# Attention scores of a two-layer decoder trunk: the matmuls of a row block regrouped by contraction depth

## The chip, the cores and the metric

The kernel runs on one core of a Trainium2 chip. The metric is the device time of one execution in microseconds (us), as the median of several runs.

## The reference, cut to what matters

Two layers work on x of 1024 tokens by 1024 features in float32. Layer 0 is a conformer convolution module with a gated feed-forward part; layer 1 is stick breaking attention with 16 heads of 64 features, then the same kind of feed-forward part. The change lies in the attention:

```
scale = 1 / sqrt(64); ts = arange(1024)
for each block of 128 queries, first query t0, for each head:
    z = einsum('qd,kd->qk', qblk, kh) * scale
    mask = ts[None, :] < (t0 + arange(128))[:, None]
    log_1m = where(mask, log_sigmoid(-z), 0)
    rev = cumsum of log_1m over later keys
    a = where(mask, exp(log_sigmoid(z) + rev - log_1m), 0)
    out = a @ v
```

## The kernel before, in words

To keep float32 accuracy, every operand of a matmul is split in a high and a low part. A product of a projection is three matmuls (`mm3`, L137 to L139): high by high, high by low, low by high. For the scores z, the queries of a head stand in one tile `q` of 128 partitions, the 64 high parts in one half, the 64 low parts in the other. The keys stand in `kh` (high parts in both halves) and in `kl` (low parts of both heads of a pair, each head in its own half). So one chunk of z, 128 queries by up to 512 keys, takes two matmuls on L739: one over 128 partitions (`q` by `kh`, both parts of q against the high part of k) and one over 64 partitions (the high half of `q` by `kl`). I call them the 128-row and the 64-row matmul. On the chunk with the diagonal a third one, L742, adds minus 1e30 where a key isn't earlier than its query; it multiplies two bfloat16 tiles of 128 by 128 (`identb`, `maskb`).

One call of `z_row` makes the scores of one block of 128 queries, in the tile `big` of two banks, 512 columns each. In the first half of the queries (blocks 0 to 3, up to 512 keys) it takes both heads of a pair, one bank for each: a two-head row. In the second half (blocks 4 to 7, 640 to 1024 keys) it takes one head with two chunks: a single-head row. There are 8 head pairs, so 32 two-head rows and 64 single-head rows. Behind the matmuls come two sigmoids on ScalarE (L755, L756), a scan over the keys on VectorE (L758) and a product on GpSimd (L760). `weigh` then transposes the weights on TensorE (L773), splits them into the tile `hl` (L776 and the helper L86; NH such tiles) and multiplies them with the values (L778, L779), which ends in `o` (L781, L782) and a store to DRAM (L800).

The work goes by units of a head pair and a half; the weighing runs two units behind the scores. The projections of the next head pair (L137 to L139) are put between as filling work, and in the last two steps the output projection `wo` of the first half. After the last unit, `wo` of the second half loads the stored results (L632), casts them (L633) and loads its weights (L130).

The order on each engine isn't written out by hand: a scheduler lays it out from the program with a timing model and packs the tiles into memory, so a change in one place can move instructions in the whole attention.

Of the kernel before, what the change touches and what calls it, by code (L numbers as in the profile page):

```python
# [15 lines left out]
DRAM = bass.MemoryType.DRAM  # L16

P = 128
# [3 lines left out]
HALF = 512  # L22
# [16 lines left out]
NM = 15  # L39
NH = 3  # L40
NX = 8
# [10 lines left out]
def trunk_kernel(ctx: ExitStack, tc, x, p, a_pw1_w, a_pw1_b, a_dw_w, a_dw_b, a_ln_g, a_ln_b, a_pw2_w, a_pw2_b,  # L52
# [37 lines left out]

    # ---------------------------------------------------------------- constants
    # one tile for all of them
    ctile = const.tile([P, 352], F32, name="ctile")
# [17 lines left out]
    class Rows:  # L111
        """Tiles of 4 KB, three to a slot."""

# [27 lines left out]
    def new_half():  # L141
        """High and low parts of a matrix (k, t) for the tokens of a half, in two tiles of four k blocks each."""
        return [[xtp.tile([P, 4, HALF], F32R, name="xT", align_bytes=A4) for _ in range(2)] for _ in range(2)]
# [20 lines left out]
    def ln_stats(src):  # L164
        nt = np_.tile([P, 24], F32, name="norm")
        st, mv, ve = nt[:, 0:12].rearrange("p (i s) -> p i s", i=2), nt[:, 12:14], nt[:, 14:16]
        rstd, tmp, nb = nt[:, 16:17], nt[:, 17:18], nt[:, 18:19]
        for i in range(2):
            nc.vector.bn_stats(out=st[:, i, :], in_=src[:, i * HALF:(i + 1) * HALF])
        nc.vector.bn_aggr(out=mv, in_=st)  # L170
        # reciprocal square root: a first guess from the exponent bits, then Newton steps to float32
        nc.vector.tensor_scalar(out=ve[:, 0:1], in0=mv[:, 1:2], scalar1=EPS, scalar2=None, op0=ALU.add)
        nc.vector.tensor_scalar(out=ve[:, 1:2], in0=mv[:, 1:2], scalar1=EPS, scalar2=-0.5, op0=ALU.add, op1=ALU.mult)
        nc.vector.tensor_scalar(out=tmp.bitcast(I32), in0=ve[:, 0:1].bitcast(I32), scalar1=1, scalar2=None,
                                op0=ALU.logical_shift_right)
        nc.vector.tensor_scalar(out=rstd.bitcast(I32), in0=tmp.bitcast(I32), scalar1=-1.0, scalar2=float(0x5f3759df),
                                op0=ALU.mult, op1=ALU.add)
        for _ in range(3):
            nc.vector.scalar_tensor_tensor(out=tmp, in0=rstd, scalar=ve[:, 1:2], in1=rstd, op0=ALU.mult, op1=ALU.mult)
            nc.vector.scalar_tensor_tensor(out=rstd, in0=tmp, scalar=1.5, in1=rstd, op0=ALU.add, op1=ALU.mult)  # L180
        return mv, rstd, nb
# [11 lines left out]

    # ---------------------------------------------------------------- p @ ple_w_proj, kept in DRAM until it is needed
    def ple_proj(i, sb, dst):
        """Pieces of work that need no result of the trunk."""
        pT, ws = [], []
# [36 lines left out]

    # ---------------------------------------------------------------- conv gated FFN + per-layer embedding
    def ffn_phase(i, xT, res, pp, g, b, sb, finish):
# [35 lines left out]

        # Gate and up projection: (W11 W21; W12 W22) of the two k halves and two column tiles, times (x11 x12; x21 x22) of
        # the two k halves and token halves, in seven block products (Strassen's, in Winograd's form).
        (x11, x21), (x12, x22) = ([[part[b] for part in xT[half]] for b in range(2)] for half in range(2))
# [35 lines left out]
        def fast(w, f, quad):  # L311
            """The products of column tiles f and f + 1 with all tokens, each in two parts."""
            pa, pb, pc, pd = quad
# [70 lines left out]

        # two sets of four banks
        (b0, b2), (b1, b3) = ((t[:, 0:HALF], t[:, HALF:]) for t in (big(), big()))
# [18 lines left out]

    # ---------------------------------------------------------------- layer 0
    x2d_dram = dram.tile([S, D], F32, name="x2_dram")
# [4 lines left out]
    with ExitStack() as l0:  # L412
# [3 lines left out]
        with ExitStack() as ph:  # L416
# [43 lines left out]

            # pointwise 1, the gate, and the depthwise convolution as three half-rate ones of the even, the odd and
            # the summed tokens: y_even = E + O', y_odd = B - E - O with the taps of even, odd and both places
            HB = 15 + HALF
# [18 lines left out]
            def depthwise(c, hb):  # L482
                nc.vector.tensor_tensor(out=hb[:, 2, :], in0=hb[:, 0, :], in1=hb[:, 1, :], op=ALU.add)
                # both: ACT multiplies, Pool adds. Tap k of E, O and B reads 15 - k places back.
                pb = sb.tile([P, HALF], F32, name="pb", bufs=2)
# [26 lines left out]
                yv = y.rearrange("p (m a) -> p m a", a=2)  # L512
                # the bias: in B already; E + O' takes it here
                nc.vector.scalar_tensor_tensor(out=yv[:, :, 0], in0=e, scalar=vec_a[:, 16 + c:17 + c], in1=os_[:, 0:HALF],
# [104 lines left out]

    # ---------------------------------------------------------------- output projection  # L620
    res = [None] * 8
# [30 lines left out]

    # ---------------------------------------------------------------- stick breaking attention
    with ExitStack() as ph:
# [4 lines left out]
        nc.gpsimd.memset(maskb, 0.0)  # L659
        # row q, key j of the diagonal block: NEG where j >= q  # L660
        nc.gpsimd.affine_select(out=maskb, in_=maskb, pattern=[[-1, P]], compare_op=ALU.is_gt, fill=NEG,
# [13 lines left out]
        def proj_qk(w, hp, hd):  # L675
            """q: (high | low) parts over the partitions, the other way round for the odd head.
            k: high parts twice, low parts twice."""
            is_q = w is b_wq
# [25 lines left out]
        def proj_v(qt, vs):  # L704
            """Per head (high | low) parts side by side, the other way round for odd heads."""
            cs = slice(qt * 256, (qt + 1) * 256)
# [23 lines left out]

        def z_mm(ps, at, hd, s, qb):
            n = (qb + 1) * P
            q, qs = hd["q"][s], slice(qb * P, (qb + 1) * P)
            for c0 in range(0, n, HALF):
                w = max(256, min(HALF, n - c0))
                diag = n <= c0 + HALF
                m = sides(s)[0]
                for j, (ks, k) in enumerate(((slice(0, P), hd["kh"][s]), (m, hd["kl"][0]))):
                    nc.tensor.matmul(out=ps[:, at + c0:at + c0 + w], lhsT=q[ks, qs], rhs=k[ks, c0:c0 + w],  # L739
                                     start=(j == 0), stop=(j == 1 and not diag))  # L740
                if diag:
                    nc.tensor.matmul(out=ps[:, at + n - P:at + n], lhsT=identb, rhs=maskb, start=False, stop=True)  # L742

        def z_row(hd, ss, qb, a):
            """Weight of key j: sigmoid(z_j) times the product over later keys of 1 - sigmoid(z_i) = sigmoid(-z_i);
            in the last column both parts are the mask's: 0 and 1."""
            n = (qb + 1) * P
            m = len(ss)
            ps = z_bank()
            for i, s in enumerate(ss):  # L750
                z_mm(ps, i * HALF, hd, s, qb)
            r = sb.tile([P, S], F32, name="rr", bufs=2, align_bytes=A4)
            rv, zv = (t.rearrange("p (m n) -> p m n", m=m) for t in (r, ps))
            av = a.rearrange("p (m n) -> p m n", m=m)
            nc.scalar.activation(out=av[:, :, 0:n], in_=zv[:, :, 0:n], func=AF.Sigmoid)  # L755
            nc.scalar.activation(out=rv[:, :, 0:n], in_=zv[:, :, 0:n], func=AF.Sigmoid, scale=-1.0)  # L756
            for i in range(m):
                nc.vector.tensor_tensor_scan(out=rv[:, i, 1:n][:, ::-1], data0=rv[:, i, 1:n][:, ::-1],  # L758
                                             data1=zero.broadcast_to([P, n - 1]), initial=1.0, op0=ALU.mult, op1=ALU.add)
            nc.gpsimd.tensor_tensor(out=av[:, :, 0:n - 1], in0=av[:, :, 0:n - 1], in1=rv[:, :, 1:n], op=ALU.mult)  # L760
            return av

        def weigh(hp, half, s, i, rows, o):
            """Values weighted, for head s and the four query blocks of a half."""
            v = vs[hp][s]
# [46 lines left out]
        for piece in pieces(0):  # L812
            piece()
        # the first half's units end early: its output projection goes beside the last units of the second half
        units = [(hp, half, ss) for hp in range(HP - 2) for half, ss in ((0, (0, 1)), (1, (0,)), (1, (1,)))]
# [29 lines left out]

    # ---------------------------------------------------------------- norm, layer 1 FFN
    with ExitStack() as l1:
# [45 lines left out]
```

## Time and profile before

| | us |
|---|---|
| median of 3 runs | 2754.74 (2754.44 to 2757.61) |
| span of the profiled execution, first to last instruction | 2746.3 |
| TensorE matmuls busy (PE) | 2585.2, 94% of the span |
| VectorE (DVE) | 1774.6, 65% |
| GpSimd (POOL) | 1201.6, 44% |
| ScalarE (ACT) | 1046.4, 38% |

Of the profiled execution only the span is known; the median stands 8.4 us above it, which is taken as the time around the span. Matmuls are pipelined and their ends are modelled, so a busy PE is not one at its peak: how dense the work is must be read from the starts of matmuls and of weight loads (PEld). The attention takes the stretch from 1270 to 1845 us.

### The profile page before, as it was taken

What the parts mean: (1) busy time and instruction counts of PE and PEld (TensorE: products, weight loads), DVE (VectorE), ACT (ScalarE), POOL (GpSimd) and SP (SyncE); (2) the same over time, 40 slices, a digit from 0 to 9 for tenths busy, and PEclk for the clock granted to TensorE, in tenths of its full rate; (3) what the DMA queues carried; (4) which work ended last, traced back from release to release, by engine and by line L of the source; (5) the groups of instructions that cost most, each with busy time, mean ns of one, the idle gap of its engine ahead of it and who ended that gap; (6) DMA issues with size and microseconds to landing.
All of it is one profiled execution on the core that took longest, in us unless ns stands there. A gap on an engine that the chain in (4) does not pass through costs nothing.

```text
span 2746.3 us, 34172 instructions
## 1 busy us (share of the span) xinstructions
PE 2585.2 (94%) x13300; PEld 2153.5 (78%) x13300; DVE 1774.6 (65%) x2785; ACT 1046.4 (38%) x1621; POOL 1201.6 (44%) x793
## 2 busy tenths in 40 slices
PE   8996998999999999999999999898899999999995
PEld 6885888988878778878777777588798787877874
DVE  4999769366565565583556665766946655656558
ACT  4556533233233232324555555642323332323231
POOL 3998236534434333412333333354653343433344
PEclk9998999999999999999999999999999999999998
DMA  4114421211111111222110101232221111211121
GB/s 149 47 47 153 163 68 62 77 47 61 47 54 58 52 52 46 69 92 68 32 50 23 45 25 38 73 125 89 70 69 62 47 60 48 62 46 46 47 77 61
DMA packets 149085, 179.12 MB, mean 65 GB/s; under 512 B 6508, under 2 KB 125756, under 8 KB 148924
## 3 DMA queue, kind: packets, MB, share of 16 engines
q1 hardware_dynamic: 144316, 168.56, 19.2%
q10 hardware_dynamic: 4608, 8.39, 0.8%
q8 instruction: 104, 1.70, 0.3%
q14 instruction: 57, 0.47, 0.1%
HBM read 151.76 MB, written 20.97 MB: 63 GB/s over the span
## 4 chain that ended last, share of the span: by engine, by line
PE 68%; DVE 18%; POOL 4%; issue 3%; ACT 3%; DMA 3%; SPq 0%; POOLq 0%; DVEq 0%; ACTq 0%
PE bank L137 13%; PE bank L138 13%; PE bank L139 12%; PE big L137 7%; PE big L139 7%; PE big L138 7%; PE big L739 3%; POOL w L86 3%; DVE bank L502 2%; DVE bank L509 2%; DVE pt L282 1%; DMA w<-in_ffn_w_up 1%; PE more L778 1%; PE more L779 1%; PE bank L773 1%
## 5 line engine op out<-in xcount | busy, mean ns | idle before, releaser
L86 POOL TENSOR_TENSOR w<-w 128x512 fp32r<-128x512 f32 (+1 forms) x444 | 755.8, 1716 | 1086.9 <-ACT w L299 675.8
L137 PE MATMUL bank<-w,xT 128*128 128x256 f32 x1280 | 367.2, 289 | 29.8 <-ACT sg L258 22.7
L299 ACT CAST w<-w 128x512 fp32r<-128x512 f32 x308 | 180.1, 619 | 542.0 <-DVE w L294 147.6
L138 PE MATMUL bank<-w,xT 128*128 128x256 f32 x1280 | 366.1, 287 | 1.4 <-POOL w L86 1.4
L139 PE MATMUL bank<-w,xT 128*128 128x256 f32 x1280 | 365.9, 288 | 0.9 <-DVE xT L86 0.9
L760 POOL TENSOR_TENSOR res<-res,rr 128x639 f32<-128x639 f32 (+3 forms) x96 | 150.2, 1565 | 316.2 <-DVE rr L758 290.0
L758 DVE TENSOR_TENSOR_SCAN rr<-rr,ctile 128x127 f32<-128x127 f32 (+7 forms) x128 | 180.1, 1428 | 162.2 <-ACT rr L756 162.1
L137 PEld LDWEIGHTS bank<-w,xT 128*128 128x128 f32 x1280 | 248.9, 195 | 32.6 <-ACT sg L258 24.1
L138 PEld LDWEIGHTS bank<-w,xT 128*128 128x128 f32 x1280 | 249.8, 195 | 2.5 <-POOL w L86 2.1
L139 PEld LDWEIGHTS bank<-w,xT 128*128 128x128 f32 x1280 | 248.5, 195 | 1.9 <-DVE xT L86 1.5
L132 ACT CAST w<-w 128x1024 fp32r<-128x1024 f32 x136 | 142.6, 1049 | 240.5 <-PE bank L138 42.8
L137 PE MATMUL big<-xT,w 128*128 128x512 f32 x544 | 212.0, 390 | 0.0
L138 PE MATMUL big<-xT,w 128*128 128x512 f32 x544 | 211.9, 389 | 0.0
L139 PE MATMUL big<-xT,w 128*128 128x512 f32 x544 | 211.6, 389 | 0.0
L137 PE MATMUL bank<-xT,w 128*128 128x512 f32 x496 | 197.4, 398 | 0.7 <-DVE m L86 0.6
L139 PE MATMUL bank<-xT,w 128*128 128x512 f32 x496 | 196.0, 395 | 0.0
L138 PE MATMUL bank<-xT,w 128*128 128x512 f32 x496 | 195.7, 394 | 0.0
L294 DVE TENSOR_TENSOR w<-w 128x512 f32<-128x512 f32 x176 | 126.9, 741 | 100.2 <-POOL w L86 50.4
L383 DVE TENSOR_TENSOR m<-m,bank 128x512 f32<-128x512 f32 x192 | 128.8, 682 | 85.0 <-PE bank L139 84.9
L137 PE MATMUL bank<-w,f 128*128 128x512 f32 x448 | 170.5, 395 | 7.7 <-ACT f L366 4.3
L138 PE MATMUL bank<-w,f 128*128 128x512 f32 x448 | 176.1, 393 | 0.0
L139 PE MATMUL bank<-w,f 128*128 128x512 f32 x448 | 173.2, 390 | 0.0
(161 smaller groups left out, 5969.4 us busy)
## 6 DMA issues: line engine op xcount, KB each, us to landing
w<-in_ffn_w_gate SPq DMA_DIRECT2D x44, 512.0 KB
w<-in_ffn_w_up SPq DMA_DIRECT2D x44, 512.0 KB
w<-in_ffn_w_down SPq DMA_DIRECT2D x44, 512.0 KB
w<-in_a_pw_w SPq DMA_DIRECT2D x32, 512.0 KB
pp<-o ACTq DMA_DIRECT2D x32, 256.0 KB
w<-in_ple_w_gate SPq DMA_DIRECT2D x16, 512.0 KB
w<-pp SPq DMA_DIRECT2D x16, 512.0 KB
w<-in_b_wo SPq DMA_DIRECT2D x16, 512.0 KB
```

The lines of the kernel that those rows point to most:

```text
L86: eng.tensor_tensor(out=l, in0=full, in1=h.bitcast(F32), op=ALU.subtract)
L132: nc.scalar.copy(out=h[:, 0:n], in_=raw)
L137: nc.tensor.matmul(out=o, lhsT=sh, rhs=mh, start=first, stop=False)
L138: nc.tensor.matmul(out=o, lhsT=sh, rhs=ml, start=False, stop=False)
L139: nc.tensor.matmul(out=o, lhsT=sl, rhs=mh, start=False, stop=last)
L294: nc.vector.tensor_tensor(out=out, in0=a, in1=c, op=op)
L299: nc.scalar.copy(out=h, in_=full)
L383: nc.vector.tensor_tensor(out=rv, in0=rv, in1=ps, op=ALU.add)
L502: nc.vector.scalar_tensor_tensor(out=e, in0=v, scalar=w, in1=e, op0=ALU.mult, op1=ALU.add)
L739: nc.tensor.matmul(out=ps[:, at + c0:at + c0 + w], lhsT=q[ks, qs], rhs=k[ks, c0:c0 + w], start=(j == 0), stop=(j == 1 and not diag))
L758: nc.vector.tensor_tensor_scan(out=rv[:, i, 1:n][:, ::-1], data0=rv[:, i, 1:n][:, ::-1], data1=zero.broadcast_to([P, n - 1]), initial=1.0, ...
L760: nc.gpsimd.tensor_tensor(out=av[:, :, 0:n - 1], in0=av[:, :, 0:n - 1], in1=rv[:, :, 1:n], op=ALU.mult)
```

## The change: 128-row matmuls of a row block first, then the 64-row ones

`z_mm` is now called once for a row block and goes over its two chunks twice: first the 128-row matmul of each chunk, with the mask right behind it, then the 64-row matmul of each. The same matmuls are done, on the same data, into the same banks. NH, the number of `hl` tiles of 4 KB a partition, goes from 3 to 4. Comments also go; the lines after them move by one or two (L739 becomes L737 and L743, L742 becomes L740).

```diff
-NH = 3
+NH = 4
...
-        def z_mm(ps, at, hd, s, qb):
+        def z_mm(ps, hd, ss, qb):
+
             n = (qb + 1) * P
-            q, qs = hd["q"][s], slice(qb * P, (qb + 1) * P)
-            for c0 in range(0, n, HALF):
-                w = max(256, min(HALF, n - c0))
-                diag = n <= c0 + HALF
+            qs = slice(qb * P, (qb + 1) * P)
+            chunks = [(i * HALF, s, c0, max(256, min(HALF, n - c0))) for i, s in enumerate(ss) for c0 in range(0, n, HALF)]
+            for at, s, c0, w in chunks:
+                nc.tensor.matmul(out=ps[:, at + c0:at + c0 + w], lhsT=hd["q"][s][:, qs], rhs=hd["kh"][s][:, c0:c0 + w],
+                                 start=True, stop=False)
+                if n <= c0 + HALF:
+                    nc.tensor.matmul(out=ps[:, at + n - P:at + n], lhsT=identb, rhs=maskb, start=False, stop=False)
+            for at, s, c0, w in chunks:
                 m = sides(s)[0]
-                for j, (ks, k) in enumerate(((slice(0, P), hd["kh"][s]), (m, hd["kl"][0]))):
-                    nc.tensor.matmul(out=ps[:, at + c0:at + c0 + w], lhsT=q[ks, qs], rhs=k[ks, c0:c0 + w],
-                                     start=(j == 0), stop=(j == 1 and not diag))
-                if diag:
-                    nc.tensor.matmul(out=ps[:, at + n - P:at + n], lhsT=identb, rhs=maskb, start=False, stop=True)
+                nc.tensor.matmul(out=ps[:, at + c0:at + c0 + w], lhsT=hd["q"][s][m, qs], rhs=hd["kl"][0][m, c0:c0 + w],
+                                 start=False, stop=True)
...
-            for i, s in enumerate(ss):
-                z_mm(ps, i * HALF, hd, s, qb)
+            z_mm(ps, hd, ss, qb)
```

In the order of TensorE, a single-head row before (the first of 640 keys; `big_81` is the scores' tile, `m` the keys and queries, `masks` the two mask tiles) is this, where of each "x2" the first is the 128-row and the second the 64-row matmul:

```order
L773 MATMUL more_9492<-ctile,res 128x128
L739 MATMUL big_81<-m 128x512 x2
L739 MATMUL big_81<-m 128x256 x2
L742 LDWEIGHTS masks
L742 MATMUL big_81<-masks 128x128
L137 MATMUL bank_82<-w,xT 128x256
```

And the same row now:

```order
L774 MATMUL more_9492<-ctile,res 128x128
L737 MATMUL big_81<-m 128x512
L737 MATMUL big_81<-m 128x256
L740 LDWEIGHTS masks
L740 MATMUL big_81<-masks 128x128
L743 MATMUL big_81<-m 128x512
L743 MATMUL big_81<-m 128x256
L137 MATMUL bank_82<-w,xT 128x256
```

The two 64-row matmuls (L743) now stand behind each other, and the mask has moved ahead of them. A two-head row before (384 keys for each of two heads):

```order
L739 MATMUL big_81<-m 128x384 x2
L742 LDWEIGHTS masks
L742 MATMUL big_81<-masks 128x128
L739 MATMUL big_81<-m 128x384 x2
L742 LDWEIGHTS masks
L742 MATMUL big_81<-masks 128x128
L773 MATMUL bank_84<-ctile,res 128x128
```

And a two-head row now (256 keys):

```order
L737 MATMUL big_81<-m 128x256
L740 LDWEIGHTS masks
L740 MATMUL big_81<-masks 128x128
L737 MATMUL big_81<-m 128x256
L740 LDWEIGHTS masks
L740 MATMUL big_81<-masks 128x128
L743 MATMUL big_81<-m 128x256 x2
L137 MATMUL bank_83<-xT,w 128x512
```

Over the whole attention TensorE's order goes from a 128-row to a 64-row matmul or back 384 times before and 192 times now; all 192 64-row matmuls stand in 96 pairs, and nothing stands between the two of a pair. Between the last L779 and the first transposes of the next part (L152) stand 174 matmuls of `wo` before, and 112 now. At that place SP's queue held this before (L800 stores a unit's result, L632 loads the results of the second half back, L130 loads weights):

```order
L800 DMA o_dram_94<-o 64x512
L130 DMA w<-in_b_wo 128x4x256 x2
L800 DMA o_dram_94<-o 64x512
L632 DMA w<-o_dram_94 128x2x512 x4
L130 DMA w<-in_b_wo 128x4x256 x8
```

And now:

```order
L801 DMA o_dram_94<-o 64x512
L130 DMA w<-in_b_wo 128x4x256
L632 DMA w<-o_dram_94 128x2x512 x3
L801 DMA o_dram_94<-o 64x512
L632 DMA w<-o_dram_94 128x2x512
L130 DMA w<-in_b_wo 128x4x256 x8
```

Three of the four loads now stand ahead of the last store instead of behind it.

## Rows read from the trace of the kernel before

**Rows 1.** The page: the span, and busy time by engine.
```profile
span 2746.3 us, 34172 instructions
PE 2585.2 (94%) x13300; PEld 2153.5 (78%) x13300; DVE 1774.6 (65%) x2785; ACT 1046.4 (38%) x1621; POOL 1201.6 (44%) x793
```

**Rows 2.** Busy time in the attention: PE, PEld, DVE, ACT, POOL; granted clock, DMA.
```profile
1270.00:1845.00 575.00, 555.74 (x2952) 425.42 (x2951) 352.99 (x475) 315.76 (x552) 213.85 (x121) 0.97 0.17 50
```

**Rows 3.** Groups by form, attention, PE: count, busy us, mean ns, idle before.
```profile
L739 PE MATMUL big<-m 64*128 64x512 f32 x96 | 48.8, 508 | 0.0
L742 PE MATMUL big<-masks 128*128 128x128 bf16 x128 | 29.6, 231 | 0.0
L739 PE MATMUL big<-m 64*128 64x256 f32 x64 | 24.8, 387 | 0.0
L739 PE MATMUL big<-m 64*128 64x384 f32 x32 | 14.3, 447 | 0.0
```

**Rows 4.** Timeline of weight loads, a single-head row: start, us, idle before.
```profile
1512.13 0.19 PEld L739 LDWEIGHTS big<-m 128*128 128x128 f32 x1
1512.67 0.18 PEld L739 LDWEIGHTS big<-m 64*128 64x128 f32 x1 [0.35 <-issue]
1513.10 0.19 PEld L739 LDWEIGHTS big<-m 128*128 128x128 f32 x1 [0.24 <-issue]
1513.41 0.18 PEld L739 LDWEIGHTS big<-m 64*128 64x128 f32 x1
1513.72 0.10 PEld L742 LDWEIGHTS <-masks 128*128 128x128 bf16 x1
1513.85 0.19 PEld L137 LDWEIGHTS bank<-xT,w 128*128 128x128 f32 x1
```

**Rows 5.** Timeline of matmuls at three places: start and us.
```profile
1278.63 0.59 PE L739 MATMUL big<-m 128*128 128x256 f32 x2
...
1512.13 0.39 PE L138 MATMUL bank<-xT,w 128*128 128x512 f32 x1
1512.35 1.44 PE L739 MATMUL big<-m 128*128 128x512 f32 x4
...
1843.08 0.28 PE L779 MATMUL more<-hl,m 128*128 128x256 f32 x1
1843.20 0.22 PE L778 MATMUL more<-hl,m 128*128 128x128 f32 x1
1843.26 0.34 PE L139 MATMUL bank<-w,xT 128*128 128x256 f32 x1
```

**Rows 6.** Timeline of weight loads, end of the two-head row from 1278.63.
```profile
1279.15 0.51 PEld L739 LDWEIGHTS big<-m 128*128 128x128 f32 x2
1279.91 0.19 PEld L138 LDWEIGHTS bank<-xT,w 128*128 128x128 f32 x1
```

**Rows 7.** A late stretch: all engines as in rows 2; then L742 alone (PE, PEld).
```profile
1680.00:1820.00 140.00, 130.51 (x640) 93.35 (x638) 103.80 (x127) 87.60 (x150) 54.48 (x32) 0.95 0.27 85
1680.00:1820.00 140.00, 8.15 (x35) 3.36 (x35) 0.95 0.27 85
```

**Rows 8.** Waits in the attention: us in total, times, longest.
```profile
PE big L739 <- ACT rr L756: 5.2, 8, 1.3
PE more L773 <- DVE hl L86: 4.4, 4, 2.0
ACT hl L776 <- PE more L779: 0.3, 1, 0.3
```

**Rows 9.** Timeline at the hand-over to the next part: SP's queue and PE.
```profile
1845.63 0.45 SPq L800 DMA_DIRECT2D o_dram<-o  x1
...
1870.71 0.58 PE L137 MATMUL bank<-w,xT 128*128 128x256 f32 x1 [4.95 <-ACT xT L633]
```

**Rows 10.** A wait of PE, and the stretch behind it, as in rows 2.
```profile
1441.06 1.11 PE L773 MATMUL more<-ctile,res 128*128 128x128 f32 x4 [1.99 <-DVE hl L86]
...
1441.00:1444.40 3.40, 3.34 (x11) 2.85 (x12) 3.34 (x6) 2.29 (x4) 0.52 (x1) 0.51 0.57 155
```

## The prediction, made before the changed kernel ran

> **What bounds the kernel now.** I read the page first: PE is busy 94% of the span, the next engine 65% [rows 1]. An average over stages proves little, so I read the windows next: in the attention, where everything that changes lies, PE is busy 555.7 of 575 us, and no other engine reaches two thirds of the stretch [rows 2]. PE waits for others there only 19.3 us. So the stage is bound by how long PE takes for its list, and the question is how dense that list is. Busy time doesn't tell, since ends are modelled and records overlap; starts do.
>
> The third view is therefore the timeline, and its starts give a rhythm. A 512-column matmul starts 0.22 us after another one, a 256-column one passes the queue in 0.12, a 128-column one in 0.06 [rows 5]. In this rhythm the weight load of the next matmul starts together with the matmul before it: the load for the first score matmul starts at 1512.13, and so does the projection matmul ahead of it [rows 4, 5]. The load is thus hidden. At the 64-row matmuls it isn't. The row that starts at 1512.35 should load its first 64-row weights at 1512.35; the load starts at 1512.67, after 0.35 us in which the load queue did nothing and no engine was waited for [rows 4]. From there to the next load, of a 128-row matmul, it is 0.43 us instead of 0.22. I read this as a price for each change between 128 and 64 rows: the matmul under way first runs out (0.32 less 0.22, so 0.10), then the load stands bare. The second part follows from the step 1512.67 to 1513.10: 0.43 less 0.22 is 0.21, which is the bare load (0.11) and the running out at its end (0.10). A change costs 0.21 us.
>
> **The change part by part.** *A single-head row before.* From the first matmul at 1512.35 to 1513.85, where the load of the second following projection matmul starts and with it, by the rhythm, the first such matmul, 1.50 us pass [rows 4, 5]. Its work in the rhythm is two times 0.22, two times 0.12 and 0.06 for the mask, 0.74. So 0.76 us are lost: 0.10 ahead of the first 64-row load, 0.21, then 0.19 twice (steps of 0.31 for 0.12), and 0.07 at the mask, which takes 0.13 instead of 0.06.
>
> *The same row now.* The two 128-row matmuls and the mask follow each other in the rhythm. Then one change (0.10 run out, 0.11 bare load), the second 64-row matmul with its load hidden under the first, and one change back (0.10, 0.11): 0.42 lost. It saves 0.34 us, and 64 rows 21.8 us.
>
> *A two-head row.* Before it takes from 1278.63 to 1279.91, 1.28 us [rows 5, 6], for work of four times 0.12 and two times 0.06, 0.60; 0.68 are lost. Now 0.42 are lost for the two changes, and the second head's 128-row load (0.11) is hidden only by the first head's mask (0.06), 0.05 more. It saves 0.21, and 32 rows 6.7 us. I use this for all widths, as the prices don't depend on the columns. The counts are those of the groups: 96 + 64 + 32 = 192 matmuls of 64 rows, two to a row [rows 3].
>
> Together 28.5 us at full clock. The mean granted clock of the stretch is 0.97 [rows 2], where PE's own steps are longer by as much: 29.4 us.
>
> *What the trace of before doesn't show* is a 64-row matmul behind another. Below, the pair costs nothing beyond the rhythm, as I took it; above, it costs a full change (0.21) in each of 96 rows, 20.2 us, which would leave 9. I take the lower end, since the row nearest in kind, a 128-row matmul behind a 128-row one, hides its load fully [rows 4, 5]. The pair of a two-head row could also run side by side, since the two heads use different halves of the partitions and different banks: then the second matmul vanishes, 0.12 to 0.22 us in 32 rows, 4 to 7 us more. No row shows such an overlap; I leave it out of the sum and in the range.
>
> The Trainium skill speaks against the hidden load: TensorE: Matmul & The Clock Gate, Part 3, "What overlaps and what doesn't", says that a weight load overlaps a matmul in flight only when it goes to another group of rows. By that, the pairs of the single-head rows, which use the same rows, would each show one bare load. For 128-row matmuls the rows here show the contrary, since those loads overlap although they use the same rows; for 64-row pairs nothing shows it yet.
>
> *NH from 3 to 4.* ScalarE waited for a free `hl` tile (its cast behind the second value matmul) once, for 0.3 us [rows 8]. So the fourth tile gives between 0 and 0.3 us; I take 0. Its use, if any, is for the scheduler.
>
> *Waits that take back some of it.* PE gets ahead by 6% of the stage, the others don't. In the late stretch, where less projection work fills the gaps, PE is already idle 9.5 of 140 us, and 35 of the 128 masks, so some 27% of the rows (8 us of the gain), lie there [rows 7]. There the scores wait for the sigmoids to free the only tile `big` (5.2 us in the whole stage) and the transposes for VectorE (4.4) [rows 8]. Ends are 0 and 8 us lost; I take 3, because PE is still busy 93% there, nearer to bound than not.
>
> *The hand-over.* Behind the last unit, `wo` of the first half covers the store and the loading back. PE ran dry there for 4.95 us until a cast by L633 [rows 9]. Now 62 matmuls fewer stand in that cover (174 less 112), 62 times 0.12 or 7.4 us; on the other hand three of four loads no longer queue behind the store, which was issued at 1845.63 [rows 9]. The ends are 7.4 us lost and 5 won; I take 0, as the cast that ended the gap also had loads behind the store.
>
> The sum is 29.4 less 3, 26.4 us. Against the profiled execution: 2746.3 less 26.4 is 2719.9, plus 8.4 around the span is 2728. The median of the runs, 2754.7, less 26.4 gives the same.
>
> **The rivals.** *The pair's second load stays bare.* For it: it is unseen. Against it: 128-row pairs. If only the 64 single-head pairs pay a change, 64 times 0.21 is 13.4 us off: gain 13, 2742. This is what the page's sentence above comes to.
>
> *More than the sum.* The two-head pairs overlap (4 to 7 us), or the late waits don't grow and the denser list leaves fewer dips of the clock: gain 34 to 40, 2715 to 2721. For the first the rows say nothing. The same page, Part 3, "Measured speedup vs the span model", has small matmuls in different groups of rows run side by side; no row of this case shows it.
>
> *The scheduler's new order hands most of it back.* The order on all engines moves throughout the attention. If the late stretch keeps nothing (8 us) and the hand-over loses its 7.4, and some waits are new, the gain is 5 to 14: 2741 to 2750.
>
> *Slower: VectorE's order collides with the weighing.* VectorE works in order; when a long scan stands ahead of the subtraction that makes `hl`, PE's transposes wait for a bank. It happened at 1441.06: PE waited 1.99 us, and then ran 3.4 us at a granted clock of 0.51, the lower of its two levels (1.2 GHz against 2.4), which costs 1.7 us more [rows 10]. So one collision costs 3.7 us. It takes eight new ones, one for each head pair, to cancel 29 us; with twelve the kernel ends 15 us slower, 2770. Against it: in the whole stage such waits for VectorE came to 4.4 us in four places [rows 8], and VectorE is busy 61% of it [rows 2].
>
> **How the numbers follow.** The sum as it stands (gain 20 to 33, 2721 to 2734): 0.53. More than the sum: 0.16. The bare second load: 0.12. Handed back: 0.11. Slower: 0.05, and 0.03 for something that cancels to within 0.2%. That 0.2%, 5.5 us, is about what a measurement of this kernel can tell from no change. The range leaves out the top of the second case (0.04), most of the handed-back one beyond 2744 (0.08) and the last two (0.08), so it goes from 2715 to 2744. Of the handed-back case 0.03 lies inside 0.2%: faster 0.53 + 0.16 + 0.12 + 0.08 = 0.89, same 0.06, slower 0.05.
>
> **What would show it.** In the changed profile, a single-head row should go from its first matmul to the restart of the rhythm in 1.16 us instead of 1.50, with one stretch of idle loads ahead of the first L743 and none ahead of the second (about 0.22 or 0.12 after it, by its width). If the second L743 load comes 0.10 later than that, the first rival holds; if the two L743 of a two-head row start within a few hundredths of a us, they overlap. The idle time on the load queue put to "issue" should halve. PE's idle time in the attention (19.3 us) should grow by some 3 us; above 30 it has handed the gain back. A wait for `hl` in every head pair would mean the slower case, and it would make the prediction wrong, as would a gap over 12 us at the hand-over.

## The result, and the profile after

The changed kernel takes 2726.16 us (median of 4 runs, 2722.46 to 2726.38) against 2754.59 for the kernel before (4 runs, 2751.79 to 2757.61): a ratio of 0.9894, with a 95% interval of 0.988 to 0.9908, so 25 to 33 us faster. The profiled execution has a span of 2720.3 us (before 2746.3); it took 2722.46 us itself, so what lies around the span is some 2 us, not the 8.4 that I took the median's distance for. By the same 2 us the profiled execution of the kernel before took some 2748 us, less than each of its four runs; so the spans differ by 26.0 us and the medians by 28.4.

The page of the changed kernel: span, and busy time by engine (against [rows 1]).

```profile
span 2720.3 us, 34159 instructions
PE 2554.6 (94%) x13300; PEld 2149.7 (79%) x13300; DVE 1785.5 (66%) x2785; ACT 1045.9 (38%) x1621; POOL 1195.0 (44%) x793
```

PE is busy for 31 us less with as many matmuls as before, and its share of the span is the same 94%. The busy time in the attention of the changed kernel, columns as in [rows 2], then its late part, as in [rows 7]:

```profile
1270.00:1822.00 552.00, 527.79 (x3011) 425.90 (x3010) 361.59 (x477) 315.64 (x552) 211.19 (x121) 0.97 0.18 55
1680.00:1822.00 142.00, 128.76 (x779) 104.89 (x780) 107.02 (x136) 85.59 (x142) 61.31 (x34) 0.95 0.31 100
```

PE now idles 24.2 us in this stage (552 less 527.79) instead of 19.3. A single-head row of the changed kernel, first the timeline of weight loads, the counterpart of [rows 4]:

```profile
1362.10 0.41 PEld L737 LDWEIGHTS big<-m 128*128 128x128 f32 x2
1362.67 0.10 PEld L740 LDWEIGHTS <-masks 128*128 128x128 bf16 x1
1362.83 0.29 PEld L743 LDWEIGHTS big<-m 64*128 64x128 f32 x2
1363.37 0.19 PEld L137 LDWEIGHTS bank<-xT,w 128*128 128x128 f32 x1 [0.25 <-issue]
1363.48 0.19 PEld L138 LDWEIGHTS bank<-xT,w 128*128 128x128 f32 x1
```

then its matmuls:

```profile
1362.10 0.39 PE L139 MATMUL bank<-xT,w 128*128 128x512 f32 x1
1362.33 0.50 PE L737 MATMUL big<-m 128*128 128x512 f32 x2
1362.67 0.23 PE L740 MATMUL big<-masks 128*128 128x128 bf16 x1
1362.83 0.61 PE L743 MATMUL big<-m 64*128 64x512 f32 x2
1363.37 0.50 PE L137 MATMUL bank<-xT,w 128*128 128x512 f32 x1
```

From the first matmul (1362.33) to the restart of the rhythm (1363.48) it is 1.15 us; the forecast was 1.16. The mask follows in the rhythm. The first 64-row load starts 0.16 us behind the mask: 0.06 for its columns, 0.10 to run out. The two 64-row loads take 0.29 us together and 0.19 each, so the second starts 0.10 behind the first, when the first matmul starts: it is hidden beneath it. Then one change back, 0.25 us of idle load queue and a bare load from 1363.37 to 1363.48.

A two-head row of the changed kernel, weight loads and then matmuls, is another matter:

```profile
1343.25 0.10 PEld L740 LDWEIGHTS <-masks 128*128 128x128 bf16 x1
1343.41 0.19 PEld L743 LDWEIGHTS big<-m 64*128 64x128 f32 x2
1343.73 0.19 PEld L139 LDWEIGHTS bank<-w,xT 128*128 128x128 f32 x1
1343.84 0.19 PEld L137 LDWEIGHTS bank<-w,xT 128*128 128x128 f32 x1
```

```profile
1342.89 0.28 PE L737 MATMUL big<-m 128*128 128x256 f32 x1
1343.01 0.23 PE L740 MATMUL big<-masks 128*128 128x128 bf16 x1
1343.05 0.36 PE L737 MATMUL big<-m 128*128 128x256 f32 x1
1343.26 0.23 PE L740 MATMUL big<-masks 128*128 128x128 bf16 x1
1343.42 0.39 PE L743 MATMUL big<-m 64*128 64x256 f32 x2
```

The two 64-row loads take 0.19 us together, as long as one, and the two matmuls 0.39. They run side by side, and each uses its own half of the partitions and its own bank. The row takes 0.95 us (1342.89 to 1343.84), where 1.07 was forecast (1.28 less 0.21). From the pair's load to the next one it is 0.32 us: 0.11 bare load, 0.11 for 256 columns once, 0.10 to run out.

### The profile page after: what moved, and what is told of

Its sections match the earlier page's. It is cut to its first block, busy times and chain, and to the rows that moved or that the text cites. A ratio compares the mean times of both kernels' runs of the same rounds, so it can differ in the third digit from the quotient of the medians.

```text
span 2720.3 us, 34159 instructions
## 1 busy us (share of the span) xinstructions
PE 2554.6 (94%) x13300; PEld 2149.7 (79%) x13300; DVE 1785.5 (66%) x2785; ACT 1045.9 (38%) x1621; POOL 1195.0 (44%) x793
## 4 chain that ended last, share of the span: by engine, by line
PE 68%; DVE 18%; POOL 4%; issue 3%; DMA 3%; ACT 3%; SPq 0%; POOLq 0%; DVEq 0%; ACTq 0%
PE bank L137 13%; PE bank L138 13%; PE bank L139 13%; PE big L137 8%; PE big L139 7%; PE big L138 7%; POOL w L86 3%; DVE bank L502 2%; DVE bank L509 2%; DVE pt L282 2%; PE big L743 1%; DMA w<-in_ffn_w_up 1%; PE bank L774 1%; PE more L779 1%; PE more L780 1%
## 5 line engine op out<-in xcount | busy, mean ns | idle before, releaser
L759 DVE TENSOR_TENSOR_SCAN rr<-rr,ctile 128x127 f32<-128x127 f32 (+7 forms) x128 | 186.9, 1481 | 121.3 <-ACT rr L757 120.9
```

## The experiments

Besides the stretch of the profile, the time of each is given as a ratio to 17 runs of the kernel before on the same chip (median 2753.29 us on the chip of the first four kernels below, 2754.11 on that of the last three). The low products over 128 partitions, in three of these kernels, add a term that doesn't belong to the scores; it is of the size of the low by low product that all kernels here leave out. Lengths of rows that stand without their lines are read in the same way, as medians over the rows between two projections at full clock; rows of one width differ by 0.03 us at most.

**The overlap taken away.** In a two-head row the second head's low product goes over 128 partitions. Against the changed kernel:

```diff
             for at, s, c0, w in chunks:
-                m = sides(s)[0]
+                m = slice(0, P) if at and len(ss) == 2 else sides(s)[0]
```

> The changed kernel, but in a two-head row the second head's low product goes over 128 partitions instead of 64 (it adds low part of q by low part of the other head's k, of the size of the product that every kernel here leaves out). The order on all engines is that of the changed kernel, and so is the number of changes between 64 and 128 rows: two in a row. Theory (the two 64-row matmuls of a two-head row run side by side and that is worth one stream each): two-head rows of 256 columns take 1.06 us instead of 0.94, those of 512 some 0.2 us more, 4.7 us over 32 rows; the time is 2730 to 2732 against 2726.2. Rival (the starts 3 ns apart are only how the records come out, the streams follow each other): rows as long as in the changed kernel, 2725 to 2727.

It took 2732.18 us (6 runs), ratio 0.9926 (0.991 to 0.9942), with a span of 2725.6, 5.3 us longer than the changed kernel's. The order on the engines is the same in both, so the two-head rows are all that differs in the program. One such row, weight loads and then matmuls:

```profile
1343.52 0.50 PEld L743 LDWEIGHTS big<-m 64*128 64x128 f32 x2
1343.94 0.19 PEld L139 LDWEIGHTS bank<-w,xT 128*128 128x128 f32 x1
1344.06 0.19 PEld L137 LDWEIGHTS bank<-w,xT 128*128 128x128 f32 x1
```

```profile
1343.00 0.28 PE L737 MATMUL big<-m 128*128 128x256 f32 x1
...
1343.53 0.70 PE L743 MATMUL big<-m 64*128 64x256 f32 x2
```

The pair now takes 0.70 us, and the row 1.06 (1343.00 to 1344.06) instead of 0.95. Rows of 384 and 512 columns are 0.17 and 0.22 us longer than in the changed kernel, and the single-head rows are as long. Over 32 rows that makes 5.0 us; of the 5.3 us of span, 4.6 lie ahead of the fourth group of transposes behind the attention. The theory holds: the overlap is real and worth about 5 us.

**No change of row count at all, in the old order.** Against the kernel before:

```diff
-                for j, (ks, k) in enumerate(((slice(0, P), hd["kh"][s]), (m, hd["kl"][0]))):
+                for j, (ks, k) in enumerate(((slice(0, P), hd["kh"][s]), (slice(0, P), hd["kl"][0]))):
```

> The kernel before, NH 3, its interleaved order, but all low products go over 128 partitions (as above, one more low by low product). So no matmul changes the number of rows; bank, weights and mask stay. Theory (the price is the change of row count, 0.21 us each, 384 times): a single-head row takes 0.8 instead of 1.50 us, a two-head row 0.7 instead of 1.28; TensorE's list is 62 to 65 us shorter, waits grow by 10 to 25 us, the time is 2698 to 2715. Rival (the price comes from two matmuls that add to one bank behind each other, or from the mask's bfloat16 weights): no change, 2750 to 2758.

It took 2706.73 us (5 runs, 2698.08 to 2715.35), ratio 0.9836 (0.9812 to 0.986). A single-head row of it, loads and then matmuls:

```profile
1358.74 0.87 PEld L739 LDWEIGHTS big<-m 128*128 128x128 f32 x4
1359.65 0.10 PEld L742 LDWEIGHTS <-masks 128*128 128x128 bf16 x1
1359.65 0.20 PEld L139 LDWEIGHTS bank<-xT,w 128*128 128x128 f32 x1
1359.77 0.19 PEld L137 LDWEIGHTS bank<-xT,w 128*128 128x128 f32 x1
```

```profile
1358.96 0.85 PE L739 MATMUL big<-m 128*128 128x512 f32 x4
```

Four matmuls on the same two banks in the same order as in [rows 4], and the row takes 0.81 us (1358.96 to 1359.77) instead of 1.50. The banks and the bfloat16 mask are as before, so the price was that of the row count. The row saves 0.69 us for four changes, 0.17 each. This kernel is faster than the changed one: by the ratios (0.9836 against 0.9894) some 16 us, though the profiled spans differ by 8.5 only. Its attention, busy time as above:

```profile
1270.00:1804.00 534.00, 495.12 (x2947) 418.46 (x2947) 358.34 (x474) 315.13 (x552) 214.70 (x121) 0.98 0.18 54
```

PE's list is some 62 us shorter (0.69 in 64 rows; in 32 two-head rows 0.55, 0.73 instead of 1.28, which is 0.14 a change). PE now idles 38.9 us in the stage instead of 19.3, so 20 of the 62 went into new waits.

**Both together: grouped and no change of row count.**

```diff
-                nc.tensor.matmul(out=ps[:, at + c0:at + c0 + w], lhsT=hd["q"][s][m, qs], rhs=hd["kl"][0][m, c0:c0 + w],
+                nc.tensor.matmul(out=ps[:, at + c0:at + c0 + w], lhsT=hd["q"][s][:, qs], rhs=hd["kl"][0][:, c0:c0 + w],
```

> The changed kernel, NH 4, but all low products over 128 partitions. Theory: with no change of row count, grouping is worth nothing more; within 6 us of the kernel before with all products over 128 partitions, 2695 to 2715. Rival (grouping has a worth of its own, fewer turns between banks): 8 us or more below that one.

It took 2711.16 us (4 runs, 2710.04 to 2712.17), ratio 0.985 (0.9833 to 0.9868). The intervals of the two overlap; without changes of row count the grouping gives nothing that could be measured.

**NH alone.**

```diff
-NH = 3
+NH = 4
```

> The kernel before with NH 4 alone; the scheduler's order changes with it. Theory (the fourth tile and the new order give nothing): 2749 to 2760. Rival (part of the 28 us came from it): 2735 to 2748.

It took 2748.85 us (12 runs), ratio 0.999 (0.9975 to 1.0006): no change that could be measured, though the order moved on all engines. The forecast of 0 for this edit stands.

**The mask's place alone.** Against the changed kernel, so that the 64-row matmul of a chunk follows its mask:

```diff
-            for at, s, c0, w in chunks:
                 m = sides(s)[0]
```

> The mask moved between the 128-row and the 64-row matmul of its chunk, nothing else: the row count changes 384 times as before; NH 4. Theory (only the changes count): a row as long as before within 0.1 us, 2748 to 2760. Rival (the mask's load and its place behind the 64-row matmul are part of what was saved, 0.07 us a mask or more): 2735 to 2746.

It took 2749.37 us (12 runs), ratio 0.9991 (0.9978 to 1.0005). A two-head row of 256 columns, its first matmul and then the loads behind it:

```profile
1342.27 0.28 PE L737 MATMUL big<-m 128*128 128x256 f32 x1
```

```profile
1343.56 0.19 PEld L137 LDWEIGHTS bank<-w,xT 128*128 128x128 f32 x1
1343.67 0.19 PEld L138 LDWEIGHTS bank<-w,xT 128*128 128x128 f32 x1
```

It takes 1.40 us (1342.27 to 1343.67), where it took 1.28 before; a single-head row takes 0.05 us more than before. So the place of the mask by itself saves nothing: with as many changes of the row count, the rows got a little longer.

**One kind of row at a time.** `z_old` is `z_mm` of the kernel before.

```diff
...
-            z_mm(ps, hd, ss, qb)
+            if len(ss) == 1:
+                z_mm(ps, hd, ss, qb)
+            else:
+                for i, s in enumerate(ss):
+                    z_old(ps, i * HALF, hd, s, qb)
```

> Grouping in the 64 single-head rows alone; two-head rows keep the interleaved order; NH 4. 256 changes of row count instead of 384. Theory (each row saves what the changed trace shows, 0.35 to 0.42 us a single-head row): TensorE's list is 24 us shorter than before, waits take 2 to 6 of it, 2730 to 2740. Rival (the single-head rows lie beside waits and their saving is handed back, the gain is the two-head rows'): 2745 to 2756.

It took 2730.53 us (6 runs), ratio 0.992 (0.9904 to 0.9935): 24 us, as the theory said. With `len(ss) == 2`:

> Grouping in the 32 two-head rows alone; single-head rows keep the interleaved order; NH 4. 320 changes instead of 384. Theory (0.35 to 0.45 us a row, of which 0.12 to 0.23 is the overlap of the pair): the list is 12 us shorter, 2740 to 2748; with the run above the two gains add up to 28 plus or minus 6. Rival: 2750 to 2757, or the same gain as the run above.

It took 2737.28 us (6 runs), ratio 0.9939 (0.9924 to 0.9954): 17 us, more than the 6 to 15 that were expected, and the two add up to 40, not to 28. Here the expectation missed. The profiles don't show this excess in the attention. Its stretch, up to the fourth group of transposes behind it, with two-head rows alone and then with single-head rows alone:

```profile
1270.00:1880.50 610.50, 585.51 (x3243) 461.58 (x3241) 392.35 (x551) 326.85 (x567) 225.55 (x125) 0.96 0.18 55
```

```profile
1270.00:1871.50 601.50, 570.56 (x3222) 459.63 (x3221) 395.37 (x550) 326.15 (x565) 223.86 (x125) 0.95 0.20 61
```

And the same stretch of the kernel before and of the changed kernel:

```profile
1270.00:1888.70 618.70, 591.84 (x3229) 460.61 (x3227) 387.44 (x549) 326.47 (x565) 224.48 (x125) 0.97 0.18 53
```

```profile
1270.00:1859.50 589.50, 557.02 (x3227) 454.02 (x3225) 395.33 (x549) 326.69 (x565) 223.24 (x125) 0.96 0.19 56
```

Against the 618.7 us of before, two-head rows alone save 8.2 us, single-head rows alone 17.2, and both together 29.2: singly they add up to less, not to more. The idle time of PE would speak for an excess of 3.4 us (against before it grew by 4.1 with single-head rows alone, fell by 1.9 with two-head rows alone, and grew by 5.6 with both), but the granted clock differed too between these executions (0.97 before, 0.96 and 0.95 singly, 0.96 with both). Each of the three gains is known to some 4 us only, so a part of the excess of 12 can be chance; where the rest comes from stays open.

## Why the prediction came out

Forecast were 2728 us, 2715 to 2744, and a gain of 26.4; measured were 2726.16, and a gain of 28.4 by the medians and 26.0 by the spans. By its steps:

- **The stage is bound by PE's list.** Right: each kernel with fewer changes of row count is faster, and those with as many (NH alone, the mask alone) are not.
- **A change of row count costs 0.21 us.** The cause is right, and shown by the kernel without any change: a single-head row falls from 1.50 to 0.81. The size holds in the changed row, where two changes lose 0.41 us against the rhythm (1.15 less 0.74), but not for all: the four changes of the old row cost 0.69, so 0.17 each, and those of a two-head row 0.14 each. The row without any change still takes 0.07 more than its 0.74 in the rhythm, which is what the prediction counted as lost at the mask. The load queue's idle time put to "issue" in the attention fell from 66.3 to 35.3 us, by about half, as the prediction asked. The Trainium skill, TensorEngine Tiling, Key Properties, says that a change of the tiling mode drains TensorE, and a change of tile alone doesn't; the trace agrees, with 0.10 us to run out at each change between 128 and 64 rows, none between two pieces of 64, and it adds that the next load lies bare behind it (0.11).
- **A single-head row saves 0.34.** Right: 1.15 us, so 0.35.
- **A two-head row saves 0.21.** Mis-sized: 0.33 at 256 columns, 0.40 at 384 and 0.45 at 512. The step that failed is "I leave it out of the sum": the overlap of the pair, which only the range held. It saves one stream, 0.11 us at 256 columns as read above and in proportion 0.16 at 384 and 0.21 at 512. The four rows of a head pair have 256, 256, 384 and 512 columns, 0.59 us together, and 8 pairs 4.7; the run without it, where rows were 0.11 to 0.22 longer, was 5.3 us of span slower. The Trainium skill's sentence, in TensorE: Matmul & The Clock Gate, Part 3, that small matmuls in different groups of rows run side by side, is borne out: 0.39 us for two matmuls.
- **The second load of a pair is hidden.** Right: it starts 0.10 behind the first, not the 0.22 or 0.12 that the prediction named, since the first load is itself bare. Here the rule of the Trainium skill on the same page, Part 3, that a load overlaps only a matmul in another group of rows, is not what the trace shows: the two of a single-head row use the same rows. The rival built on it (2742) falls.
- **Waits take back 3 us.** Mis-sized, but small: PE's idle time in the stage grew by 4.9 us, and by 5.6 up to the fourth group of transposes behind it. (PE gets ahead by 29.4 of 575 us, which is 5%, not the 6% that the prediction wrote; nothing hangs on it.) The idle time came where the forecast looked for it, in the transposes and value matmuls that wait for VectorE. The waits of PE in the changed kernel's attention (in all, times, longest; three of 1.5 us and less left out):

```profile
PE more L780 <- DVE hl L86: 6.6, 10, 1.0
PE more L779 <- DVE o L783: 4.5, 5, 1.3
PE bank L774 <- DVE hl L86: 2.9, 3, 1.7
PE bank L138 <- POOL w L86: 2.4, 1, 2.4
PE big L737 <- ACT rr L757: 2.2, 3, 0.8
PE more L774 <- DVE hl L86: 1.8, 2, 1.6
```

  And of before, those for VectorE beside the 4.4 us of [rows 8]:

```profile
PE more L779 <- DVE hl L86: 3.5, 5, 1.6
PE more L778 <- DVE o L782: 3.4, 6, 0.8
PE bank L773 <- DVE hl L86: 1.2, 3, 0.5
```

  So these waits for VectorE grew from 12.5 to 15.8 us; the prediction, which put them at 4.4 in four places, had counted one group of four. None of them is longer than 1.7 us now, so the slower rival, a collision for each head pair, didn't come. The longest wait, 2.4 us, is a single one for GpSimd in the projections. The wait for the sigmoids fell from 5.2 us [rows 8] to 2.2.
- **The hand-over gives and takes nothing.** Nearly right. The last store was issued at 1823.19, 22 us earlier than in [rows 9], and PE ran dry for 6.71 us instead of 4.95, behind the same cast:

```profile
1823.19 0.45 SPq L801 DMA_DIRECT2D o_dram<-o  x1
```

```profile
1843.18 0.58 PE L137 MATMUL bank<-w,xT 128*128 128x256 f32 x1 [6.71 <-ACT xT L633]
```

  From that store to the end of the gap it is 19.99 us, and before it was 25.08 (1845.63 to 1870.71): 5.1 us sooner, with 7.4 us of covering work less. PE's dry time there grew by 1.8 us.

The sum with the measured sizes: 28.5 and 4.7 make 33.2 us, at the clock of 0.97 34.2. In the stretch from 1270 us to the fourth group of transposes, shown above for both kernels, PE's busy time fell by 34.8 us (591.84 to 557.02) and its idle time grew by 5.6, the hand-over included; that leaves 29.2. Behind it, in a part that the change doesn't touch, the changed kernel took 3.2 us more (last section), and so the span gained 26.0. That the forecast of 26.4 came so near is thus partly luck: an overlap left out (4.7 us), waits and hand-over set 2.6 too low, and 3.2 us from elsewhere about cancel.

## What to carry to other kernels

When TensorE bounds a stage, read the starts of its weight loads: where a load doesn't start with the matmul before it and nothing is waited for, look at what changes between the two matmuls. Here it was the change between 128 and 64 contraction rows. Each cost 0.14 to 0.21 us, so the two changes around a lone 64-row matmul cost more than its own stream of 0.12 to 0.22. Grouping halves the changes. Making the small matmul as tall as the others removes them and was worth some 16 us more, where the operands allow it and the small term that it adds can be borne. Two 64-row matmuls on different halves of the partitions and different banks, put behind each other, took as long as one.

## What I had not expected

The parts of the program that no edit touches weren't equally long. From the fourth group of transposes behind the attention to the end, the order hardly differs between kernels, yet it took 857.6 us before, 860.8 in the changed kernel, and 851.4 with the mask moved alone. The three stretches, one from each profile in this order:

```profile
1888.70:2746.30 857.60, 802.85 (x4004) 680.33 (x4004) 532.58 (x820) 250.57 (x364) 375.57 (x248) 0.98 0.18 59
```

```profile
1859.50:2720.30 860.80, 805.75 (x4014) 682.69 (x4014) 534.62 (x821) 249.67 (x364) 369.62 (x248) 0.98 0.18 59
```

```profile
1894.40:2745.80 851.40, 800.37 (x4002) 678.33 (x4000) 529.32 (x819) 249.90 (x364) 375.90 (x248) 0.98 0.18 59
```

The granted clock is 0.98 in all three, but two digits hide a part. By the trace's clock records, TensorE was at the lower of its two levels for 17.1 us of this stretch before, 20.5 in the changed kernel and 13.7 with the mask moved alone, up to the last matmul. If work at half the clock takes twice as long, an estimate, the clock makes at most 1.7 of the 3.2 us between the first two, and 3.4 of the 9.4 between the last two. What makes the rest stays open.

The same scatter stands between runs of one kernel. Of the 17 runs of the kernel before on the second chip, the two with the lowest mean granted clock (0.969) took 2759.7 and 2762.2 us, the four with the highest (0.974) 2745.3 to 2753.4. This bounds how finely times of such kernels can be added and subtracted.
